# First four chunks of the hidden layer plain instead of two, and other places for the sums of squares

## Chip, cores and metric

The kernel runs on one core of one Trainium2 chip. The metric is the device time of one execution in microseconds (us), lower is better. Engines: TensorE (PE, its weight loads PEld), VectorE (DVE), ScalarE (ACT), GpSimd (POOL), SyncE (SP, which issues all DMAs here).

## What is computed

A decoder trunk on 512 tokens with model width 1024, in float32. Two layers; each has a SwiGLU feed-forward network (FFN) before and one after its mixer. The first mixer is a multi-scale causal pooling, the second a multi-head latent attention that reads one shared latent K/V. All reads of the residual h go through an RMSNorm.

```
def swiglu(u, wg, wu, wd):
    return (jax.nn.silu(u @ wg) * (u @ wu)) @ wd
...
    for l in range(DEPTH):
        h = h + 0.5 * swiglu(rmsnorm(h, ffn_pre_norm[l]), ...)
        u = rmsnorm(h, mix_norm[l])
        h = h + (pool_mixer(u, ...) if l < N_A_LAYERS else mla_attention(u, ...))
        h = h + 0.5 * swiglu(rmsnorm(h, ffn_post_norm[l]), ...)
        if l == N_A_LAYERS - 1:
            k_nope, k_rope, v = mla_shared_kv(h, ...)
    return rmsnorm(h, final_norm)
```

## The kernel before

Everything is kept transposed: h is eight tiles of 128 channels x 512 tokens. Each float32 product is made of three fp32r matmuls (`mm3`, lines 115 to 119): high by high, high by low, low by high part. So each weight is cast to its high part on ACT (L144, L178) and subtracted to its low part on DVE (L145, L179), and each input is split in the same way: high on ACT (L303), low on DVE (L308).

**RMSNorm.** The gain goes into the split of h; the root of the mean square is applied afterwards, to the products. `Norm.square` makes squares on ACT (the last one on DVE, L318), `Norm.accumulate` adds them on POOL into `sq_acc` (L325). `token_sums` (L239) sums over the partitions on TensorE: sixteen matmuls of one column, first operand `sq_acc`, then `sq`. `rsqrt` (L250 to L257) is eleven tiny instructions on DVE. `on_all` makes a diagonal on DVE (L280), spreads it over all partitions by a matmul of 512 columns (L287), and ACT copies it to `rb` (L289). `norm.r()` is sums and root, `norm.spread(r)` is `on_all`.

**FFN.** The hidden width 2816 is 22 chunks of 128. The first N_FIRST = 2 chunks are "plain": eight channels of input times gate and up weights (four products of 512 columns and 128 channels per channel, weights in four units of 512 KB, `wfirst`), accumulated in four PSUM tiles. From chunk 2 on, a chunk's gate and up product is made Strassen-like, with seven products of half size (p1 to p7: 84 matmuls of 256 columns). `group_weights` loads two tiles (`wgu`) and forms the sums of weight blocks with four additions on POOL (L191), splitting four tiles on the way; the split tiles come from `wsplit` (four buffers, shared with `load_w`), `wb` (two) and `wf` (two). The input side needs the operands `t1`, `t2`, `t4` (`Quarters.prepare`, L382 to L407) and `t3` (`prepare_t3`, L400 to L407), which overwrites the right half of the first four channels' split inputs; so it must come after the last plain product that reads these. p4 and p3 of a chunk run in the next chunk's loop.

`gated` (plain) or `p3` (Strassen) gives the hidden activation, which is split and kept (`mids`, eight chunks). The down product takes four chunks at a time: `down_steps(g)` says which columns d of the output are made in the loop of chunk g, `early` (between p2 and p4) or `late` (behind p7). `down_tail` is the rest. `DOWN_ORDER` fixes the order of the weights in memory. `on_h` is called when an output column is final; it starts the next norm's splits and squares.

TensorE's order is that of the program inside `manual_schedule`; the order of all other engines, and of TensorE outside, comes from a planner that simulates the program.

**Where the sums stand before.** In an FFN, behind the first of the four units (two channels): sums and root; behind the second: the spread and t3. In the pool stage (line 635): behind all four products of the first pair. Shared K/V (line 692): sums, root and spread by the planner's order, in front of `shared_kv`. At the end: the last two output columns are made in two token halves; behind the first half come its sums, root, spread, eight products on POOL (L942) and four DMAs, behind the second half sums, transposes and output.

Of the kernel before, what the change touches and what calls it, by code (L numbers as in the profile page):

```python
# [16 lines left out]
P = 128  # L17
T = 512
D = 1024
# [3 lines left out]
HT = T // 2  # L23
N_FIRST = 2
PART = 4
# [17 lines left out]
def down_steps(g):  # L43


    i, base = g % PART, g - g % PART - PART
    if base < 0:
        return [], []
    most, end, whole = range(base, base + PART - 1), [base + PART - 1], range(base, base + PART)
    if i == 0:  # L50
        return [], [(d, most, True, False) for d in range(2)]
    early = [(d, end, False, True) for d in range(2)] if i == 1 else []
    return early, [(d, whole, True, True) for d in (2 * i, 2 * i + 1)]
# [15 lines left out]
def trunk_kernel(  # L69
# [36 lines left out]
    def f(ap):  # L106
        return ap.bitcast(F32)
# [309 lines left out]

    def ffn(idx, norm, on_h, first=None, last=False):
        with tc.tile_pool(name="mid", bufs=1) as midp, tc.tile_pool(name="wb", bufs=2) as wb, \
# [108 lines left out]
            for u in range(ND // 2):  # L528
# [4 lines left out]
                if u == 0:  # L533
                    r = norm.r()
                    quarters = norm.quarters
                    quarters.prepare(ND // 2 - 1)
                elif u == 1:
                    rb = norm.spread(r)
                    for k in range(ND // 2):
                        quarters.prepare_t3(k)  # L540
            for j in range(2):
                gated(j, ps[2 * j], ps[2 * j + 1])

# [32 lines left out]
            for th in range(2 if last else 0):  # L576
                for step in down_tail()[-2:]:
                    down(*step, ts=slice(th * HT, (th + 1) * HT))


# [11 lines left out]
    with tc.tile_pool(name="pool", bufs=1) as pp:  # L592
# [41 lines left out]
        with tc.manual_schedule(engines={mybir.EngineType.PE}):  # L634
            os = {(0, tb): product(0, tb) for tb in range(NQB)}
            r = rms(norm.squares, D)
            for tb in range(2):
# [20 lines left out]

    def shared_kv(mean, rb):
        w = [part(load_w(wdkv[u]), 4, 256) for u in range(2)]  # L660
        o, orope = mm_tile(), mm_tile()
        with tc.tile_pool(name="kvw", bufs=2) as kw:
            for c in range(ND):
                x = split_gain(h[c], G_KV, c, kw, "kvh")
                mm3(o, [a[:, c % 4, :P] for a in w[c // 4]], x, c == 0, c == ND - 1)
                mm3(orope, [a[:, c % 4, P:] for a in w[c // 4]], x, c == 0, c == ND - 1)
            kr = kw.tile([P, T], F32, tag="kvr", name="kvr", bufs=1)
# [18 lines left out]
            nc.vector.tensor_tensor(out=krl[:64], in0=kr[:64], in1=f(krh[:64]), op=ALU.subtract)  # L686
            nc.sync.dma_start(f(krh[64:]), f(krh[:64]))

    class Shared:


        def __init__(self, norm):
            mean = mean_of(token_sums(norm.squares), D)
            self.base, self.gh, self.quarters = norm.base, norm.gh, norm.quarters
            self.rb = on_all(rsqrt(mean, "rms_r"))
            shared_kv(mean, self.rb)

# [236 lines left out]
    hg = [None] * ND  # L934

    def first_half():

        rb = final.rb(slice(0, half))
        for c in range(0, ND, 2):
# [22 lines left out]
    def on_h(c, ts):  # L962
        final.add(c, ts)
        if ts.start == 0:
            hg[c] = resid.tile([P, T], F32, tag=f"gh{c}_hi", name=f"hg{c}")
        nc.scalar.mul(hg[c][:, ts], h[c][:, ts], gain(G_FIN, c))
        if c == ND - 1:
            (second_half if ts.start else first_half)()

    ffn(3, norm, on_h, last=True)  # L970
    room.close()

# [92 lines left out]
```

## Time and profile before

| | |
|---|---|
| median of 2 runs | 1816.7 us (1815.43 to 1817.96) |
| profiled execution | 1818.21 us, its span 1816.4 us |
| mean granted TensorE clock | 0.974 of 2.4 GHz |
| TensorE busy, its weight loads | 95%, 86% |
| DVE, ACT, POOL busy | 73%, 48%, 34% |
| mean DMA rate | 92 GB/s |

In a row, the first figures are start and duration in us (timeline) or busy time and mean ns of one (groups); in brackets stands the idle time of the engine before the instruction and what ended it. A matmul's listed duration overlaps the next one's; the distance between starts is the pace.

### The profile page before, as it was taken

What the parts mean: (1) busy time and instruction counts of PE and PEld (TensorE: products, weight loads), DVE (VectorE), ACT (ScalarE), POOL (GpSimd) and SP (SyncE); (2) the same over time, 40 slices, a digit from 0 to 9 for tenths busy, and PEclk for the clock granted to TensorE, in tenths of its full rate; (3) what the DMA queues carried; (4) which work ended last, traced back from release to release, by engine and by line L of the source; (5) the groups of instructions that cost most, each with busy time, mean ns of one, the idle gap of its engine ahead of it and who ended that gap; (6) DMA issues with size and microseconds to landing.
All of it is one profiled execution on the core that took longest, in us unless ns stands there. A gap on an engine that the chain in (4) does not pass through costs nothing.

```text
span 1816.4 us, 28079 instructions
## 1 busy us (share of the span) xinstructions
PE 1725.0 (95%) x11088; PEld 1570.9 (86%) x11088; DVE 1329.3 (73%) x2121; ACT 869.1 (48%) x1428; POOL 610.0 (34%) x424
## 2 busy tenths in 40 slices
PE   4999999996999999989999999999999889999997
PEld 3899999985999999978999999878887679999996
DVE  8677777678777777789777777787665867777774
ACT  5444444454444444454444444576664534444443
POOL 4333333224333333233333332412121323333322
PEclk7999999998999999999999999999999889999998
DMA  4233333321233333222333333321221123333321
GB/s 151 86 101 105 105 105 105 105 84 34 94 105 105 105 101 99 93 70 87 105 105 105 105 105 99 94 69 52 83 82 47 58 82 105 104 100 99 97 90 48
DMA packets 49590, 166.83 MB, mean 92 GB/s; under 512 B 6320, under 2 KB 6320, under 8 KB 49456
## 3 DMA queue, kind: packets, MB, share of 16 engines
q1 hardware_dynamic: 49456, 165.02, 28.6%
q8 instruction: 87, 1.43, 0.3%
q14 instruction: 47, 0.39, 0.1%
HBM read 158.44 MB, written 2.10 MB: 88 GB/s over the span
## 4 chain that ended last, share of the span: by engine, by line
PE 86%; DVE 9%; ACT 2%; issue 2%; POOL 1%; DMA 1%; SPq 0%; DVEq 0%; POOLq 0%; ACTq 0%
PE mm L117 20%; PE mm L119 20%; PE mm L118 20%; PE aux L117 7%; PE aux L118 7%; PE aux L119 7%; DVE wlo L179 1%; DVE gh_lo L308 1%; DVE t_lo L407 1%; DVE wlo L145 1%; PE mm L831 1%; DVE b L401 1%; PE mm L830 1%; PE aux L867 1%; PE mm L832 0%
## 5 line engine op out<-in xcount | busy, mean ns | idle before, releaser
L191 POOL TENSOR_TENSOR wraw<-wraw 128x512 f32<-128x512 f32 x320 | 482.3, 1508 | 803.9 <-DVE flo L179 689.7
L117 PE MATMUL mm<-gh_hi,whi 128*128 128x256 f32 (+1 forms) x1424 | 425.9, 299 | 7.6 <-ACT whi L144 7.5
L118 PE MATMUL mm<-gh_lo,whi 128*128 128x256 f32 (+1 forms) x1424 | 423.5, 297 | 0.0
L119 PE MATMUL mm<-gh_hi,wlo 128*128 128x256 f32 (+1 forms) x1424 | 422.6, 297 | 0.0
L178 ACT CAST whi<-wraw 128x1024 fp32r<-128x1024 f32 x240 | 252.0, 1051 | 251.1 <-POOL wraw L191 205.4
L179 DVE TENSOR_TENSOR wlo<-wraw,whi 128x1024 fp32r<-128x1024 f32 x240 | 297.7, 1242 | 32.0 <-ACT whi L178 31.8
L117 PEld LDWEIGHTS mm<-gh_hi,whi 128*128 128x128 f32 x1424 | 276.2, 194 | 18.3 <-ACT whi L144 7.5
L118 PEld LDWEIGHTS mm<-gh_lo,whi 128*128 128x128 f32 x1424 | 275.8, 194 | 10.6 <-issue 1.5
L119 PEld LDWEIGHTS mm<-gh_hi,wlo 128*128 128x128 f32 x1424 | 275.4, 193 | 7.2 <-issue 0.2
L117 PE MATMUL aux<-mh,whi 128*128 128x512 f32 x576 | 225.3, 391 | 0.0
L118 PE MATMUL aux<-ml,whi 128*128 128x512 f32 x576 | 225.2, 391 | 0.0
L119 PE MATMUL aux<-mh,wlo 128*128 128x512 f32 x576 | 224.1, 389 | 0.0
L119 PE MATMUL mm<-t_hi,wlo 128*128 128x256 f32 x640 | 184.1, 288 | 10.1 <-DVE wlo L179 10.1
L474 DVE TENSOR_TENSOR mm<-c,mm 128x256 f32<-128x256 f32 x80 | 34.2, 428 | 207.4 <-PE mm L119 207.4
L117 PE MATMUL mm<-t_hi,whi 128*128 128x256 f32 x640 | 183.6, 287 | 0.0
L118 PE MATMUL mm<-t_lo,whi 128*128 128x256 f32 x640 | 183.5, 287 | 0.0
L145 DVE TENSOR_TENSOR wlo<-wraw,whi 128x1024 fp32r<-128x1024 f32 (+2 forms) x142 | 164.3, 1157 | 22.8 <-ACT whi L144 22.4
L144 ACT CAST whi<-wraw 128x1024 fp32r<-128x1024 f32 (+2 forms) x172 | 145.5, 863 | 55.9 <-PE mm L118 31.4
L432 ACT COPY c<-mm 128x256 f32<-128x256 f32 x240 | 88.6, 370 | 130.1 <-PE mm L119 130.1
L119 PEld LDWEIGHTS mm<-t_hi,wlo 128*128 128x128 f32 x640 | 125.4, 196 | 10.9 <-DVE wlo L179 10.9
L487 DVE TENSOR_TENSOR gate<-gate,rb 128x512 f32<-128x512 f32 x88 | 130.4, 1482 | 3.5 <-ACT gate L486 3.5
L119 PEld LDWEIGHTS aux<-mh,wlo 128*128 128x128 f32 x576 | 108.2, 188 | 23.2
(209 smaller groups left out, 3428.8 us busy)
## 6 DMA issues: line engine op xcount, KB each, us to landing
wraw<-in_wgu SPq DMA_DIRECT2D x160, 512.0 KB, 3.6
wraw<-in_wd SPq DMA_DIRECT2D x88, 512.0 KB, 3.6
wraw<-in_wo SPq DMA_DIRECT2D x16, 512.0 KB, 3.7
wraw<-in_wfirst SPq DMA_DIRECT2D x12, 512.0 KB, 3.6
wraw<-in_wheads SPq DMA_DIRECT2D x8, 512.0 KB, 3.5
h<-in_xT SPq DMA_DIRECT2D x8, 256.0 KB, 5.4
wraw<-in_wfirst SPq DMA_DIRECT2D x8, 256.0 KB, 5.4
qr<-yh SPq DMA_DIRECT2D x32, 64.0 KB, 2.0
```

The lines of the kernel that those rows point to most:

```text
L117: nc.tensor.matmul(out, w[0], x[0], start=start, stop=False, **kw)
L118: nc.tensor.matmul(out, w[0], x[1], start=False, stop=False, **kw)
L119: nc.tensor.matmul(out, w[1], x[0], start=False, stop=stop, **kw)
L144: nc.scalar.copy(hi[:, s], raw[:, s])
L145: lo_engines[i % len(lo_engines)].tensor_tensor(out=lo[:, s], in0=raw[:, s], in1=f(hi[:, s]), op=ALU.subtract)
L178: nc.scalar.copy(hi[:, s], raw[:, s])
L179: nc.vector.tensor_tensor(out=lo[:, s], in0=raw[:, s], in1=f(hi[:, s]), op=ALU.subtract)
L191: nc.gpsimd.tensor_tensor(out=out, in0=x, in1=y, op=ALU.add)
L308: nc.vector.scalar_tensor_tensor(out=lo, in0=h[c], scalar=gain(self.base, c), in1=f(hi), op0=ALU.mult, op1=ALU.subtract)
L432: nc.scalar.copy(t, acc[g]["x"])
L474: nc.vector.tensor_tensor(out=y, in0=act[g]["c16"], in1=y, op=ALU.add)
L487: nc.vector.tensor_tensor(out=gate, in0=gate, in1=rb, op=ALU.mult)
```

## The change

N_FIRST becomes 4: chunks 2 and 3 are plain too, with weights from the `wgu` units of these chunks (the up weights' two halves of channels lie in swapped order there). Chunk 2 is done gate first, then up; chunk 3 "by channel", gate and up alternating. Sums and root stand behind all eight channels of chunks 0 and 1, the spread behind chunk 2's gate, `gated` of chunks 0 and 1 with it; t3 is prepared when chunk 3 is through channel 3. The first down columns' first three chunks, `late` in chunk 4 before, become `early` there. In the pool stage the sums stand behind two of four products. `shared_kv` gets its own manual order with the sums behind channel 4. At the end, the first half's sums stand behind column 6 of the second half (`last`), its spread and output behind the last column.

```diff
-N_FIRST = 2
+N_FIRST = 4
...
-    if base < 0:
-        return [], []
     most, end, whole = range(base, base + PART - 1), [base + PART - 1], range(base, base + PART)
     if i == 0:
-        return [], [(d, most, True, False) for d in range(2)]
+        steps = [(d, most, True, False) for d in range(2)]
+        return (steps, []) if base == 0 else ([], steps)
...
                 if u == 0:
-                    r = norm.r()
                     quarters = norm.quarters
                     quarters.prepare(ND // 2 - 1)
-                elif u == 1:
+            r = norm.r()
+            ws = [part(load_w(wgu[idx, 0, m]), ND, P) for m in range(2)]
+            for m in range(2):
+                o = mm_tile()
+                for c in range(ND):
+                    mm3(o, [x[:, (c + 4 * m) % ND] for x in ws[m]], norm.gh[c], c == 0, c == ND - 1)
+                ps.append(o)
+                if m == 0:
                     rb = norm.spread(r)
+                    for j in range(2):
+                        gated(j, ps[2 * j], ps[2 * j + 1])
+            gated(2, ps[4], ps[5])
+
+            ws = [part(load_w(wgu[idx, 1, m]), ND, P) for m in range(2)]
+            ps = [mm_tile() for _ in range(2)]
+            for c in range(ND):
+                for m in range(2):
+                    mm3(ps[m], [x[:, (c + 4 * m) % ND] for x in ws[m]], norm.gh[c], c == 0, c == ND - 1)
+                if c == ND // 2 - 1:
                     for k in range(ND // 2):
                         quarters.prepare_t3(k)
-            for j in range(2):
-                gated(j, ps[2 * j], ps[2 * j + 1])
+            gated(3, *ps)
...
                     down(*step, ts=slice(th * HT, (th + 1) * HT))
+                    if th == 1 and step[0] == ND - 2:
+                        last()
...
-            os = {(0, tb): product(0, tb) for tb in range(NQB)}
-            r = rms(norm.squares, D)
+            os = {(0, tb): product(0, tb) for tb in range(2)}
+            ss = token_sums(norm.squares)
+            os.update({(0, tb): product(0, tb) for tb in range(2, NQB)})
+            r = rsqrt(mean_of(ss, D), "rms_r")
...
-            for c in range(ND):
-                x = split_gain(h[c], G_KV, c, kw, "kvh")
-                mm3(o, [a[:, c % 4, :P] for a in w[c // 4]], x, c == 0, c == ND - 1)
-                mm3(orope, [a[:, c % 4, P:] for a in w[c // 4]], x, c == 0, c == ND - 1)
+            with tc.manual_schedule(engines={mybir.EngineType.PE}):
+                for c in range(ND):
+                    x = split_gain(h[c], G_KV, c, kw, "kvh")
+                    mm3(o, [a[:, c % 4, :P] for a in w[c // 4]], x, c == 0, c == ND - 1)
+                    mm3(orope, [a[:, c % 4, P:] for a in w[c // 4]], x, c == 0, c == ND - 1)
+                    if c == 4:
+                        mean = mean_of(token_sums(norm.squares), D)
+            rb = on_all(rsqrt(mean, "rms_r"))
...
+    def first_sums():
+        firsts.append(final.r(slice(0, half)))
     def first_half():
-        rb = final.rb(slice(0, half))
+        rb = on_all(firsts.pop())
...
-        if c == ND - 1:
-            (second_half if ts.start else first_half)()
+        if c == ND - 1 and ts.start:
+            first_half()
+            second_half()
```

## Rows read from the trace of the kernel before

**Rows 1.** The page, busy us, share of the span and instructions of each engine.
```profile
PE 1725.0 (95%) x11088; PEld 1570.9 (86%) x11088; DVE 1329.3 (73%) x2121; ACT 869.1 (48%) x1428; POOL 610.0 (34%) x424
```

**Rows 2.** Waits of TensorE: us in total, times, longest us.
```profile
PE aux L239 <- POOL sq_acc L325: 28.7, 5, 12.3
...
PE aux L239 <- DVE sq L318: 17.8, 4, 6.2
...
PE aux L287 <- DVE diag L280: 10.9, 5, 4.3
...
PE mm L119 <- DVE wlo L179: 10.1, 4, 2.6
...
PE mm L117 <- DVE pvl L359: 4.4, 1, 4.4
```

**Rows 3.** Timeline of TensorE, head of FFN 0.
```profile
7.51 0.79 PE L117 MATMUL mm<-gh_hi,whi 128*128 128x512 f32 x1 [7.51 <-ACT whi L144]
...
27.32 0.59 PE L239 MATMUL aux<-ones,sq_acc 128*128 128x1 f32 x2 [12.30 <-POOL sq_acc L325]
...
36.54 0.77 PE L117 MATMUL mm<-gh_hi,whi 128*128 128x512 f32 x1
...
46.34 1.12 PE L287 MATMUL aux<-diag,ones 128*128 128x512 f32 x2 [1.51 <-DVE diag L280]
...
58.23 0.28 PE L117 MATMUL mm<-gh_hi,whi 128*128 128x256 f32 x1
...
68.30 0.28 PE L117 MATMUL mm<-t_hi,fhi 128*128 128x256 f32 x1
```

**Rows 4.** Timeline of TensorE, FFN 3: first and 24th plain, first Strassen matmul.
```profile
1427.67 0.39 PE L117 MATMUL mm<-gh_hi,whi 128*128 128x512 f32 x1
...
1432.88 0.39 PE L119 MATMUL mm<-gh_hi,wlo 128*128 128x512 f32 x1
...
1470.89 0.28 PE L117 MATMUL mm<-gh_hi,whi 128*128 128x256 f32 x1
```

**Rows 5.** Timeline of TensorE, FFN 1: first plain and first Strassen matmul.
```profile
412.11 0.45 PE L117 MATMUL mm<-gh_hi,whi 128*128 128x512 f32 x1
...
454.87 0.28 PE L117 MATMUL mm<-gh_hi,whi 128*128 128x256 f32 x1
```

**Rows 6.** Costliest groups by form: busy us, mean ns, idle before.
```profile
L191 POOL TENSOR_TENSOR wraw<-wraw 128x512 f32<-128x512 f32 x320 | 482.3, 1508 | 803.9 <-DVE flo L179 689.7 <-DVE wlo L179 45.0 <-issue 34.2
...
L179 DVE TENSOR_TENSOR wlo<-wraw,whi 128x1024 fp32r<-128x1024 f32 x240 | 297.7, 1242 | 32.0 <-ACT whi L178 31.8
```

**Rows 7.** Timeline of DVE, heads of FFN 0, 1 and 3.
```profile
30.39 0.68 DVE L145 TENSOR_TENSOR wlo<-wraw,whi 128x512 fp32r<-128x512 f32 x1
...
42.71 1.21 DVE L255 TENSOR_TENSOR rms_t<-rms_r,mean 128x4 f32<-128x4 f32 x1
...
44.34 0.16 DVE L255 TENSOR_TENSOR rms_t<-rms_r,mean 128x4 f32<-128x4 f32 x1
...
428.44 0.74 DVE L308 SCALAR_TENSOR_TENSOR gh_lo<-h,g_sb,gh_hi 128x512 fp32r<-128x512 f32 x1
...
1442.19 0.74 DVE L308 SCALAR_TENSOR_TENSOR gh_lo<-h,g_sb,gh_hi 128x512 fp32r<-128x512 f32 x1
```

**Rows 8.** Timeline of TensorE, FFN 2: shared K/V sums, first Strassen matmul.
```profile
786.72 0.59 PE L239 MATMUL aux<-ones,sq_acc 128*128 128x1 f32 x2 [5.43 <-POOL sq_acc L325]
...
825.17 0.28 PE L117 MATMUL mm<-gh_hi,whi 128*128 128x256 f32 x1
```

**Rows 9.** Stretches: busy us of each engine, granted clock, DMA share, GB/s.
```profile
58.20:90.00 31.80, 29.16 (x230) 28.93 (x229) 23.18 (x33) 14.29 (x23) 12.31 (x8) 0.95 0.26 84
...
384.00:412.00 28.00, 23.59 (x187) 23.27 (x186) 21.73 (x37) 17.00 (x27) 5.15 (x4) 0.94 0.31 97
```

**Rows 10.** Timeline of TensorE and POOL, tail of the kernel.
```profile
1798.51 1.22 PE L287 MATMUL aux<-diag,ones 128*128 128x256 f32 x2 [2.95 <-DVE diag L280]
...
1800.22 5.57 POOL L942 TENSOR_TENSOR y<-hg,rb 128x256 f32<-128x256 f32 x8 [6.84 <-ACT rb L289]
```

More of the change, by code (lines that the diff above doesn't have):

```diff
@@ L416, in operand, with ffn @@
             return [x[:, half * HT:(half + 1) * HT] for x in tiles]
-    def ffn(idx, norm, on_h, first=None, last=False):
+    def ffn(idx, norm, on_h, first=None, last=None):
         with tc.tile_pool(name="mid", bufs=1) as midp, tc.tile_pool(name="wb", bufs=2) as wb, \
@@ L657, in trunk_kernel, with shared_kv @@
     nc.gpsimd.memset(f(krl[64:]), 0.0)
-    def shared_kv(mean, rb):
+    def shared_kv(norm):
         w = [part(load_w(wdkv[u]), 4, 256) for u in range(2)]
@@ L687, in shared_kv @@
             nc.sync.dma_start(f(krh[64:]), f(krh[:64]))
+        return rb
     class Shared:
         def __init__(self, norm):
-            mean = mean_of(token_sums(norm.squares), D)
             self.base, self.gh, self.quarters = norm.base, norm.gh, norm.quarters
-            self.rb = on_all(rsqrt(mean, "rms_r"))
-            shared_kv(mean, self.rb)
+            self.rb = shared_kv(norm)
         def r(self):
@@ L934, in trunk_kernel @@
     hg = [None] * ND
+    firsts = []
+    def first_sums():
+        firsts.append(final.r(slice(0, half)))
     def first_half():
-        rb = final.rb(slice(0, half))
+        rb = on_all(firsts.pop())
         for c in range(0, ND, 2):
@@ L966, in on_h @@
         nc.scalar.mul(hg[c][:, ts], h[c][:, ts], gain(G_FIN, c))
-        if c == ND - 1:
-            (second_half if ts.start else first_half)()
-    ffn(3, norm, on_h, last=True)
+        if c == ND - 1 and ts.start:
+            first_half()
+            second_half()
+    ffn(3, norm, on_h, last=first_sums)
     room.close()
```

## Prediction

> **What bounds the kernel now.** I read the page's busy shares first: TensorE is busy for 95% of the span [rows 1], so only its idle time and its extra columns can move the end. Next the waits of TensorE: almost all of its waiting is with a few causes, each hit once per stage [rows 2]. The token sums wait for the accumulated squares on POOL (28.7 us) and for the last square on DVE (17.8), the spreading product waits for its diagonal (10.9), weights for the channel products arrive late (10.1), and the pool stage waits once (4.4). Together 71.9 us. Then TensorE's timeline at the head of each FFN shows what such a wait costs in full. In FFN 0 the sums begin at 27.32 after 12.30 us idle, the next products start at 36.54, the spreading product at 46.34, and the 96 products of the first two chunks, begun at 7.51, are through at 58.23 [rows 3].
>
> Two spacings are needed. From 1427.67 to 1432.88 lie 23 steps between 512-column matmuls [rows 4]: 0.2265 us each. From 58.23 to 68.30 lie the 84 matmuls of one Strassen chunk, 256 columns each [rows 3]: 0.120 us each. So 96 products of 512 columns need 21.7 us. Measured were 50.7 in FFN 0 (58.23 - 7.51), 42.8 in FFN 1 (454.87 - 412.11) [rows 5] and 43.2 in FFN 3 (1470.89 - 1427.67) [rows 4]. The excess is 29.0, 21.1 and 21.5 us. Of it some 2.3 is work that stays in any order: sixteen small matmuls of the sums and the two of the spread. 26.7, 18.8 and 19.2 us, together 64.7, are waits and the half-speed clock after them.
>
> **The change part by part.**
>
> *Chunks 2 and 3 plain.* A plain chunk is 48 matmuls by 0.2265 = 10.87 us, a Strassen chunk 84 by 0.120 = 10.08. Two chunks in four FFNs: 8 x 0.79 = **+6.3 us**, all on TensorE's path. The Trainium skill, "TensorE: Matmul & The Clock Gate", section "Back-to-back issue gap", gives an isolated gap of N/2.4 + 2.5 ns, 215.8 and 109.2 ns here; by that the term would be 8 x 1.19 = 9.5. The rows show about 11 ns more for each matmul of either width, and the rows decide.
>
> What these chunks no longer need is off the path: per chunk two splits fewer on DVE (1.24 us each for 1024 columns) and four additions fewer on POOL (1.51 each) [rows 6]. As many weight bytes are loaded as before, four 512 KB units per FFN by SP, only without the additions. I cost this at nothing; it is the margin that lets the rest work.
>
> *The sums behind the eight channels of chunks 0 and 1, the spread behind chunk 2's gate.* This attacks the 64.7. TensorE now goes on with channels 2 to 7 as soon as their low parts are written, and reaches the sums 72 matmuls (16.3 us) later. What is late next is DVE, which makes those low parts:
> - FFN 0: the last weight split runs 30.39 to 31.07, the twelve matmuls of its channel follow, so the products end at 33.8 at best [rows 7], against 7.51 + 21.7 = 29.2. That is 4.6 us that stay; with the half-speed start and a few short gaps I leave 7.5.
> - FFN 1: the last low part is done at 429.18 [rows 7], when TensorE, from 412.11 without a stop, is at channel 6; its end at 433.8 is hardly touched. I leave 0.5.
> - FFN 3: the last low part is done at 1442.93 [rows 7]; channel 7 would be reached at 1427.67 + 84 x 0.2265 = 1446.7. Nothing stays.
> - The spread: between the end of the sums (36.54) and the spread (46.34) lay 9.8 us [rows 3], as the root's small instructions stand behind DVE's backlog. Chunk 2's gate covers 24 x 0.2265 = 5.4. Bounds per FFN: 0 (the backlog has drained, since DVE gets 16 us longer) to 4.4. I take 1.5, nearer to the lower end because three of DVE's heaviest jobs, the t3 operands, now come later still. Three FFNs: 4.5 stay.
>
> So 64.7 - 7.5 - 0.5 - 4.5 = **-52.2 us**.
>
> *FFN 2* has its sums inside the shared K/V. They wait 5.43 us there, and from 786.72 to 825.17 lie 144 products of 512 columns [rows 8]: 32.6 us plus 2.3 for sums and spread, so 3.5 is lost to the slow clock. Sums after channel 4 of K/V can save up to 8.9; but the K/V inputs need eight low parts more from the same loaded DVE before anything else can start. Bounds 0 to 8.9, I take the middle, **-4.5**.
>
> *The late weights of the channel products.* In each FFN the third Strassen group waits once on a split, 10.1 us in four [rows 2]. The stretch around it ran at 0.95 of the clock for 31.8 us [rows 9], thus 3.2 us at half speed, which costs 1.6. Four times 2.5 + 1.6 plus 0.2 each of pipeline drain: 17.3. The reason is that the third group's small block takes a buffer that the first group frees only in the second one's loop, and POOL's four additions (6.0 us) with the splits follow. Now the 24 matmuls of group 5's `late` columns stand between, 24 x 0.2265 = 5.4 us of cover for a wait of 2.6: it goes. In its place comes a new one. The early `down` of group 4 needs a unit of wd, whose split buffer only chunk 3 frees; it must be cast and split (1.24 on DVE [rows 6]; for the cast on ACT I take the same) while p1 and p2 run, 24 x 0.120 = 2.9 us, and DVE has chunk 3's gating and the t3 operands at the same time. Bounds 0 to 6 per FFN; I take 2, including the clock. Sum: 17.3 - 8.0 = **-9.3**.
>
> *Pool stage.* The sums go in front of two of the four products, so the root starts 24 x 0.120 = 2.9 us earlier and 2.9 us more of products lie behind it. The wait of 4.4 [rows 2] and the clock of 0.94 over 28 us [rows 9], worth 1.7, make 6.1 at most. DVE then leads through the eight h updates; I take **-4**.
>
> *Tail.* The spread of the first half waited 2.95 us at 1798.51; now the last column's second half runs in that time. POOL's eight products for the first half took 5.57 us from 1800.22 [rows 10] and stood before the second half's sums; afterwards they run beside the second half's root chain, which is what is late next. Bounds 0 to 5 us, I take **-3**. On that chain: with POOL busy a tiny DVE instruction took 1.21 us, after it 0.16 [rows 7]. The Trainium skill, "SBUF — State Buffer", section "Who interferes with whom", says that a DVE instruction with two SBUF inputs and a GpSimd one that reads SBUF exclude each other for a whole instruction. By that the chain would take up to 5 us more here and the tail gains nothing; the rows agree with the rule, and it is the lower bound that I use.
>
> Sum: +6.3 - 52.2 - 4.5 - 9.3 - 4 - 3 = -66.7. The profiled execution took 1818.21 us (span 1816.4 and 1.8 around it; the median of the two timed runs, 1816.7, lies 1.5 below): 1818.2 - 66.7 = 1751.5, **1752 us**.
>
> **Rivals.**
> 1. *The wait moves to the spread and to group 4.* If DVE's backlog isn't drained, the spread waits 4.4 and the clock falls again (some 2 us) in three FFNs, 19.2 instead of 4.5, and the early unit costs 5 instead of 2 in four: 14.7 + 12 = 26.7 us less gain, 1778. For it: 9.8 us from sums to spread. Against it: two plain chunks take work off DVE and POOL.
> 2. *Every wait goes.* DVE is ahead everywhere: the 4.5 and the 8.0 vanish and FFN 2 gives its 8.9: 17 us more, 1735. For it: the late rows of low parts lie ahead of TensorE's need in FFN 1 and 3. Against it: FFN 0's DVE row.
> 3. *Group 4 starves (the other side).* Before, the waiting at the head let ACT, DVE and POOL split two groups ahead. If that lead was bought by the wait, TensorE reaches groups 4 to 6 with no weights ready: each then runs at the pace of buffer release, two splits, two additions, a split, two additions, a split, about 14 us of chain (four casts and splits near 1.2 each, four additions at 1.5) for 10 us of products, beside t3 and four gatings on the same DVE. The gain is used up when this costs 66.7 / 4 = 16.7 us more per FFN than I allow; at 20 it gives 1831. For it: the two demands do meet in one stretch. Against it: the chain starts when buffers fall free in chunk 2, 11 to 16 us before group 4.
> 4. *DVE's order decides.* Only TensorE's order is written by hand. If the planner puts chunk 2's and 3's splits and the t3 work ahead of the low parts, half of the 52.2 stays: 1778.
>
> **How the numbers follow.** The forecast has 0.60 (its own range 1738 to 1770), rival 1 0.15, rival 2 0.10, rival 4 0.10, rival 3 0.05. The range 1734 to 1788 holds the forecast, rivals 1, 2 and 4 about their centres, and leaves out rival 3 and the outer tails. A change of 2% (36 us, below 1780.4 of the median) is about what a measurement of this kernel tells from no change: faster 0.83 (forecast, rival 2, most of 1 and 4), same 0.12, slower 0.05.
>
> **What would show it.** Right: no L239 row on TensorE waits over 2 us in FFN 0, 1 and 3; first channel product of FFN 1 some 47 us behind its first plain product (192 products, sums, spread), where four chunks are done; the granted clock near full in these stretches; no wait of 2.6 us on wlo in the third group. Wrong: waits of 4 us or more under L287, new waits of L117 to L119 on the wd unit or t3 in group 4, or low parts (L308) ending the waits of the plain products.

## The result, and the profile after the change

The changed kernel takes 1753.5 us (median of two runs, 1752.56 to 1754.46), 0.9652 of the kernel before, with a 95% interval of 0.9611 to 0.9694: faster, and 1.5 us from the forecast. The profiled execution took 1754.46 us with a span of 1752.7; that is 3.0 us above the 1751.5 that the prediction's sum gave for it. As will be seen, the sum came out better than its terms: some of them were off by more than 10 us, and that they cancelled was luck.

In the changed file the lines up to L521 carry a number one lower (L239 is L238, L287 is L286, L308 is L307), the last ones a number 26 higher (L942 is L968).

The page's busy times, and the row of the granted clock over 40 slices, answering to [rows 1]:

```profile
PE 1709.3 (98%) x10800; PEld 1542.9 (88%) x10800; DVE 1298.3 (74%) x2065; ACT 849.9 (48%) x1388; POOL 565.6 (32%) x392
...
PEclk9999999999999999989999999999999999999998
```

TensorE is at 98% where it was at 95. It has 288 matmuls fewer (8 chunks, 84 - 48 each), POOL 32 additions and DVE 56 instructions fewer.

The waits of TensorE (us in total, times, longest), answering to [rows 2]:

```profile
PE aux L286 <- DVE diag L279: 8.7, 3, 5.2
...
PE mm L116 <- ACT kvh_hi L347: 4.8, 1, 4.8
PE mm L117 <- DVE kvh_lo L348: 3.7, 1, 3.7
...
PE mm L118 <- DVE wlo L144: 1.6, 2, 1.2
```

Three of the four largest rows of before, the sums behind POOL, the sums behind DVE and the late weights (L179), are gone. The spread's row is smaller, but one of its waits is longer than any of before. And there is a new pair, the operands of the shared K/V (kvh).

TensorE's timeline at the sums and the spread, in FFN 0 and in FFN 3:

```profile
7.92 0.79 PE L116 MATMUL mm<-gh_hi,whi 128*128 128x512 f32 x1 [7.92 <-ACT whi L143]
...
33.57 0.28 PE L238 MATMUL aux<-ones,sq_acc 128*128 128x1 f32 x2
...
46.21 2.07 PE L286 MATMUL aux<-diag,ones 128*128 128x512 f32 x2 [5.20 <-DVE diag L279]
...
1385.51 0.39 PE L116 MATMUL mm<-gh_hi,whi 128*128 128x512 f32 x1
...
1407.27 0.28 PE L238 MATMUL aux<-ones,sq_acc 128*128 128x1 f32 x2
...
1414.63 1.12 PE L286 MATMUL aux<-diag,ones 128*128 128x512 f32 x2
```

In FFN 3 the 96 products take 21.8 us (1407.27 - 1385.51), the spacing's own 21.7, and the spread comes without a wait. In FFN 0 they take 25.7 (33.57 - 7.92), and the spread waits 5.2.

**The time by stage.** Milestones of TensorE's timeline cut both spans. A head of an FFN goes from its first plain product to the first of the 24 `late` down matmuls of group 5; the K/V and FFN 2 go from FFN 1's last tail product to the same point; the pool stage from FFN 0's last tail product to FFN 1's first; the tail begins behind the last tail product of 512 columns. The forecast column puts the prediction's steps on these stages (an FFN's share of the plain chunks is +1.58, of the late weights -2.33).

```
stage              before    after   change   forecast
start to FFN 0       7.51     7.92    +0.41      0
head of FFN 0       98.01    81.16   -16.85    -18.45
pool stage          27.61    21.95    -5.66     -4
head of FFN 1       89.83    72.28   -17.55    -17.55
K/V and FFN 2       94.75    93.86    -0.89     -5.25
attention          273.02   271.38    -1.64      0
head of FFN 3       90.50    69.18   -21.32    -18.45
tail                27.19    27.00    -0.19     -3
rest              1107.98  1107.97    -0.01      0
span              1816.40  1752.70   -63.70    -66.7
```

Nearly all of the gain, 61.4 of 63.7 us, lies where the prediction put most of it: in the heads of three FFNs and in the pool stage. FFN 2 and the tail, which were to give some 8, give nearly nothing. What attention shows is no work of the change; the last section comes to it.

### The profile page after: what moved, and what is told of

The parts are those of the page before. It is cut to its first block, busy times and chain, and to the rows that moved or that the text cites. A ratio compares the mean times of both kernels' runs of the same rounds, so it can differ in the third digit from the quotient of the medians.

```text
span 1752.7 us, 27363 instructions
## 1 busy us (share of the span) xinstructions
PE 1709.3 (98%) x10800; PEld 1542.9 (88%) x10800; DVE 1298.3 (74%) x2065; ACT 849.9 (48%) x1388; POOL 565.6 (32%) x392
## 5 line engine op out<-in xcount | busy, mean ns | idle before, releaser
L190 POOL TENSOR_TENSOR wraw<-wraw 128x512 f32<-128x512 f32 x288 | 438.4, 1522 | 776.4 <-DVE flo L178 682.3
L118 PE MATMUL mm<-gh_hi,wlo 128*128 128x256 f32 (+1 forms) x1424 | 433.7, 305 | 1.6 <-DVE wlo L144 1.6
L177 ACT CAST whi<-wraw 128x1024 fp32r<-128x1024 f32 x216 | 227.0, 1051 | 226.1 <-POOL wraw L190 184.2
L178 DVE TENSOR_TENSOR wlo<-wraw,whi 128x1024 fp32r<-128x1024 f32 x216 | 267.5, 1239 | 3.3 <-ACT whi L177 3.3
L144 DVE TENSOR_TENSOR wlo<-wraw,whi 128x1024 fp32r<-128x1024 f32 (+2 forms) x158 | 183.3, 1161 | 36.6 <-ACT whi L143 35.3
L143 ACT CAST whi<-wraw 128x1024 fp32r<-128x1024 f32 (+2 forms) x188 | 162.2, 879 | 82.5 <-PE mm L117 56.8
L118 PE MATMUL mm<-t_hi,wlo 128*128 128x256 f32 x576 | 163.0, 283 | 0.0
L117 PE MATMUL mm<-t_lo,whi 128*128 128x256 f32 x576 | 163.0, 283 | 0.0
L116 PE MATMUL mm<-t_hi,whi 128*128 128x256 f32 x576 | 163.0, 283 | 0.0
L324 POOL TENSOR_TENSOR sq_acc<-sq_acc,sq 128x512 f32<-128x512 f32 (+1 forms) x43 | 63.6, 1479 | 197.3 <-ACT sq L320 196.9
```

Source lines behind the costliest of these rows:

```text
L116: nc.tensor.matmul(out, w[0], x[0], start=start, stop=False, **kw)
L117: nc.tensor.matmul(out, w[0], x[1], start=False, stop=False, **kw)
L118: nc.tensor.matmul(out, w[1], x[0], start=False, stop=stop, **kw)
L143: nc.scalar.copy(hi[:, s], raw[:, s])
L144: lo_engines[i % len(lo_engines)].tensor_tensor(out=lo[:, s], in0=raw[:, s], in1=f(hi[:, s]), op=ALU.subtract)
L177: nc.scalar.copy(hi[:, s], raw[:, s])
```

## The experiments

Each ran on one chip together with the kernel before, which took 1818.4 to 1819.7 us there. The first run to read is the changed kernel itself.

**The changed kernel again** (no edit).

> The changed kernel again, unedited, beside the others on the same chip: ratio 0.965 to the kernel before, and the same stretches within 1 us but for the first transfers at the start (7 to 8.4 us in the other runs).

Measured: 1755.1 us, ratio 0.9646 (0.9633 to 0.9659). Every stage from FFN 0's head on lies within 0.2 us of the table; the start took 7.12. In the kernels that follow, stages that an edit does not touch differ somewhat more: by up to 0.9 us in FFN 2's, by up to 0.4 in the tail, and FFN 0's head, which begins with the first transfers, once by 1.5. So smaller differences of one stage are not read as an edit's. 0.9646 is the ratio that the others are held against.

**The sums back at their old place**, the chunks plain:

```diff
                 if u == 0:
+                    r = norm.r()
                     quarters = norm.quarters
                     quarters.prepare(ND // 2 - 1)
-            r = norm.r()
+                elif u == 1:
+                    rb = norm.spread(r)
...
                 if m == 0:
-                    rb = norm.spread(r)
                     for j in range(2):
```

> The changed kernel (four plain chunks) with the sums of FFN 0, 1 and 3 back behind channels 0 and 1 and the spread back behind channels 2 and 3. Theory: the place of the sums makes the gain: the waits under the sums' line come back and with them some 52 to 65 us: 1807 to 1819. Rival: the two plain chunks, which take splits from DVE and additions from POOL, made most of it: below 1780, with waits under the sums' line of less than half of before (46.5 us).

Measured: 1788.0 us, ratio 0.9833 (0.9817 to 0.9849), so 34 us above the changed kernel. Neither 52 us nor "most of it by the plain chunks": it fell between the two theories. The waits of TensorE in this kernel:

```profile
PE aux L238 <- POOL sq_acc L324: 17.7, 2, 11.5
PE aux L238 <- DVE sq L317: 16.9, 3, 7.2
...
PE aux L286 <- DVE diag L279: 1.8, 1, 1.8
```

The sums' waits are back, all in the three heads, with 34.6 us; before had 39.3 there (46.5 by [rows 2], less 5.4 in FFN 2 and 1.8 in the tail). The spread's are not: of 10.9 only the tail's 1.8 is left. So the plain chunks alone remove the spread's waits in the FFNs, the late weights, and a small part of the sums' waits, 4.7 us. What they remove of the spread's in the three heads is 6.7 us: the 1.5 of [rows 3] in FFN 0 and, in the kernel before, these two in FFN 1 and FFN 3:

```profile
442.98 1.12 PE L287 MATMUL aux<-diag,ones 128*128 128x512 f32 x2 [0.88 <-DVE diag L280]
...
1456.29 2.08 PE L287 MATMUL aux<-diag,ones 128*128 128x512 f32 x2 [4.26 <-DVE diag L280]
```

**The other half alone**: two plain chunks as before, the sums behind all eight channels, the spread behind the first two Strassen products.

```diff
-                    r = norm.r()
                     quarters = norm.quarters
...
-                elif u == 1:
-                    rb = norm.spread(r)
-                    for k in range(ND // 2):
-                        quarters.prepare_t3(k)
-            for j in range(2):
-                gated(j, ps[2 * j], ps[2 * j + 1])
+            r = norm.r()
...
                 p2(g)
+                if g == N_FIRST:
+                    rb = norm.spread(r)
...
```

(The last part also holds the gating of chunks 0 and 1 and the t3 operands.)

> The kernel before (two plain chunks) with one edit: sums of FFN 0, 1 and 3 behind all eight channels, spread, gating and the t3 operands behind the first two products of the first Strassen group. Theory: the sums' waits go, but only 2.9 us of products lie between sums and spread, where 9.8 are needed in FFN 0: spread waits of 5 to 8 us and the clock's fall after them, some 10 us in each of three FFNs, so half of the 52 to 57 us is kept: 1785 to 1795. Rival: no cover is needed and the plain chunks only cost their 6.3 us: 1760 to 1768. Other rival: DVE, with the operands of the Strassen products ahead of it, is late for the first group in any order, and nothing is won: 1810 or more.

Measured: 1810.3 us, ratio 0.9955 (0.994 to 0.997): 8 us won. That is the number of the "other rival", and its reason, DVE with other work ahead, is close too. The waits, and DVE's timeline in FFN 3, where the sums are through at 1445.04:

```profile
PE aux L287 <- DVE diag L280: 45.9, 5, 16.6
PE mm L119 <- DVE wlo L179: 10.1, 4, 2.6
```

```profile
1451.04 2.28 DVE L179 TENSOR_TENSOR wlo<-wraw,whi 128x1024 fp32r<-128x1024 f32 x1
1453.24 0.15 DVE L265 TENSOR_SCALAR mean<-aux 128x4 f32<-128x4 f32 x1
1455.55 1.23 DVE L179 TENSOR_TENSOR wlo<-wraw,whi 128x1024 fp32r<-128x1024 f32 x1 [2.16 <-ACT whi L178]
1456.69 0.16 DVE L250 TENSOR_SCALAR rms_t<-mean 128x4 int32<-128x4 int32 x1
```

The sums' waits are gone in the three heads, and nearly their whole price is paid one step later, at the spread. DVE keeps the order it was given: the mean stands behind t3 operands and weight splits for 8.2 us (1453.24 - 1445.04), and then a split, itself waiting 2.16 us for ACT, stands between the mean and the root's first instruction. The third group's late weights stay, with 10.1.

The three heads in the four kernels, from the same milestones:

```
                                FFN 0    FFN 1    FFN 3    sum against before
before                          98.01    89.83    90.50
plain chunks, sums early        92.86    84.51    80.34    -20.6
two plain, sums late            96.10    87.88    87.32     -7.0
changed kernel (both)           81.16    72.28    69.18    -55.7
```

The two parts alone make 27.7 us, together 55.7. The half that is missing belongs to neither. DVE's timeline above shows why: the late sums need the shorter queues that the plain chunks make. One thing more differs: between sums and spread lie 24 products of 256 columns here (2.9 us) and 24 of 512 in the changed kernel (5.4). That accounts for at most 7.7 us in the three heads, where the spread waits 41.7.

**Which queue?** The prediction costed what the plain chunks take off POOL and DVE at nothing. In FFN 3's head of before, DVE's groups by shape (busy us, mean ns) hold this row:

```profile
L308 DVE SCALAR_TENSOR_TENSOR gh_lo<-h,g_sb,gh_hi 128x512 fp32r<-128x512 f32 x4 | 5.0, 1254 | 0.0
```

With four plain chunks and early sums the same four instructions read:

```profile
L307 DVE SCALAR_TENSOR_TENSOR gh_lo<-h,g_sb,gh_hi 128x512 fp32r<-128x512 f32 x4 | 2.9, 739 | 0.0
```

The mean of the same work is 0.5 us shorter; in before two of the four take 0.74 us as here, and two take 1.75 and 1.79. What is missing beside it is POOL's additions for the Strassen groups: in before, six of them lie between 1431.77 and 1451.96, 8.5 us in all. So the next kernel puts POOL work back into the kernel of the sums' old place, 12 additions in each of three FFNs whose result goes nowhere:

```diff
...
+                    for _ in range(3 if c >= ND // 2 and idx != 2 else 0):
+                        nc.gpsimd.tensor_tensor(out=scrap, in0=scrap, in1=f(norm.gh[c][0])[:, :256], op=ALU.add)
...
```

> The kernel with four plain chunks and the sums at their old place (1788.0 us in the earlier run, ratio 0.983), with 12 additions of 128x256 on POOL that nobody needs at the head of FFN 0, 1 and 3, some 0.7 us each, so about 8.6 us of POOL in each, about as much as the two Strassen groups' additions put there before. Theory: a good part of what the plain chunks win beside their own price is that these additions are gone, which stand ahead of the squares on POOL and beside which DVE's small blocks take up to twice as long: the heads of the three FFNs (92.9, 84.5 and 80.3 us) grow by 3 to 8 us each, and the time is 1797 to 1810. Rival: what counts is DVE's own shorter list (fewer splits, t3 later), and POOL has room: each head within 1.5 us of these values, 1788 to 1792.

Measured: 1805.6 us, ratio 0.9925 (0.9908 to 0.9941), 17 us more. POOL's and DVE's groups, the first over the whole run, the second from 1421.3 to 1442.0 in FFN 3:

```profile
L535 POOL TENSOR_TENSOR scrap<-scrap,gh_hi 128x256 f32<-128x256 f32 x36 | 36.4, 1011 | 2.0
```

```profile
L309 DVE SCALAR_TENSOR_TENSOR gh_lo<-h,g_sb,gh_hi 128x512 fp32r<-128x512 f32 x4 | 3.8, 975 | 0.0
```

12.1 us of POOL work in each head made the heads 5.5, 6.6 and 3.8 us longer (98.32, 91.11 and 84.16), 15.9 together, and DVE's blocks grew from 0.739 to 0.975 us in the mean. The sums' waits rose from 34.6 to 51.8 us:

```profile
PE aux L240 <- DVE sq L319: 29.1, 3, 11.4
PE aux L240 <- POOL sq_acc L326: 22.7, 3, 14.2
```

So additions on POOL do lengthen these waits, and most of the 17.2 us more, 12.2, is waiting for the last square, which DVE makes. But the 15.9 us are not a share of the 20.6 that the plain chunks had won by themselves: this load is larger than before's and lies at other moments, and the sums' waits now exceed before's 39.3, of which the plain chunks had taken only 4.7. The spread did not start to wait, so POOL does not make that part. What is left as its cause is DVE's own list, which the plain chunks shorten; no run takes that alone.

**The place of the early down steps.**

```diff
-        return (steps, []) if base == 0 else ([], steps)
+        return [], steps
```

> The changed kernel with one word of the order taken back: the first down steps of the fifth group stand behind its seven products, not between its second and third. Theory: the third group's wait went because the late columns stand ahead of it, and the early place costs and brings nothing: 1754.5 within 1.5. By the step of the prediction the early unit costs 2 us in each FFN, which goes: 1747. Rival: the early place is what covers the weights of the first Strassen group, and its wait of 2.6 us with the slow clock (some 4 us each) comes back in every FFN: 1770.

Measured: 1753.9 us, ratio 0.9646 (0.9631 to 0.966): no difference. Neither the 2 us per FFN of the prediction nor the rival's cover exists; the third group's wait stays away without the early place.

**The shared K/V.**

```diff
-    def shared_kv(norm):
+    def shared_kv(mean, rb):
...
-                    if c == 4:
-                        mean = mean_of(token_sums(norm.squares), D)
-            rb = on_all(rsqrt(mean, "rms_r"))
...
```

(The sums and the spread stand ahead of the products again, and TensorE's order there is the planner's.)

> The changed kernel with the shared K/V alone taken back (sums ahead of the K/V products, spread left to the planner). By the step of the prediction the move was worth 4.5 us: 1759. By the reading of the trace the wait only changed its cause (5.43 us for the accumulated squares before, 4.78 for the first K/V operand and 3.65 for its low part after, on the same rows of ACT and DVE): 1754.5 within 1.5 either way, with a wait of some 5 us for the squares at the head of FFN 2 again.

Measured: 1753.6 us, ratio 0.9644 (0.9628 to 0.966): no difference in the time (the stage takes 92.5 us against 93.9, and attention the 1.6 more that the last section tells of). TensorE's first wait there is the old one again:

```profile
746.50 0.58 PE L238 MATMUL aux<-ones,sq_acc 128*128 128x1 f32 x2 [5.47 <-POOL sq_acc L324]
```

So the change took away a wait that hid another, of 4.8 us. ACT makes the first kvh behind the end of FFN 1's products although it needs only h. Its pool is opened where FFN 1's middle operands lay. The next kernel puts these operands into buffers that stand free:

```diff
-                    x = split_gain(h[c], G_KV, c, kw, "kvh")
+                    x = [room.act.tile([P, T], F32R, tag=tag, name=f"kvh_{s}", bufs=3) for s, tag in (("hi", "g"), ("lo", "m"))]
+                    nc.scalar.mul(x[0], h[c], gain(G_KV, c))
...
```

> The changed kernel with one edit: the two operands of each K/V product (kvh) lie in buffers that stand free (those of g and m), not in a pool opened where FFN 1's middle operands lay. Theory: in FFN 2 the waits of 4.8 and 3.6 us under the K/V products are waits for that memory, since its last readers are the last products of FFN 1; with it the operands are made beside these products and both waits go, with the slow clock behind them: the stretch from FFN 1's last tail product to FFN 2's late columns, 88.8 us, loses 6 to 10, and the time is 1745 to 1749. Rival: ACT and DVE are simply busy with FFN 2's own operands in that order, and the wait stays or moves to the sums, which wait for the last square: 1753 or more.

Measured: 1748.3 us, ratio 0.961 (0.9597 to 0.9623); the stage takes 87.5 us, 6.4 less. TensorE's timeline there, and ACT's row of the first two operands, at 745.62 in the changed kernel:

```profile
740.77 0.39 PE L116 MATMUL mm<-kvh_hi,whi 128*128 128x512 f32 x1
743.64 0.70 PE L117 MATMUL mm<-kvh_lo,whi 128*128 128x512 f32 x1 [2.48 <-DVE kvh_lo L685]
```

```profile
730.92 1.32 ACT L684 ACTIVATE kvh_hi<-h,g_sb 128x512 fp32r<-128x512 f32 x2
```

The memory was the cause: with nothing but the buffers changed, the operands are made 15 us earlier. (There are three buffers now and not two; for the first two operands that can't matter.) By which way it works is not shown: in the changed kernel FFN 1's last product ends at 741.61, and ACT, before it makes kvh at 745.62, still does a split, a square and a cast from 743.53 on, in the planner's order. What is late next is their low part, behind DVE's other work, with 2.48.

**The pool stage.**

```diff
-            os = {(0, tb): product(0, tb) for tb in range(2)}
-            ss = token_sums(norm.squares)
-            os.update({(0, tb): product(0, tb) for tb in range(2, NQB)})
-            r = rsqrt(mean_of(ss, D), "rms_r")
+            os = {(0, tb): product(0, tb) for tb in range(NQB)}
+            r = rms(norm.squares, D)
```

> The changed kernel with the pool stage alone taken back: all four products of the first pair ahead of the sums. If the edit itself made the stage's 5.6 us (27.4 us before, 21.8 after, from the last tail product to FFN 1's first product), the stage takes 27.4 again and the time is 1760. If part of it came from the emptier queues that the new FFN 0 leaves behind, the loss is 2 us or less: 1756.

Measured: 1757.1 us, ratio 0.9661 (0.9646 to 0.9675). The profiled execution, with a span of 1753.1, is at the fast end of its runs; by the ratios the edit is worth 2.7 us (0.0015 of 1818). The stage takes 25.0 us: 3.0 of its 5.7 are this edit's, of which FFN 1's head gives 1.0 back (71.25). The other 2.6 came with the rest of the change. Two plain chunks with late sums leave the stage at 28.2, and four with early sums and the pool stage's edit have it at 22.1, close to the changed kernel's 21.9, so it is the plain chunks'. By which engine wasn't tried.

**The tail.**

```diff
...
-        if c == ND - 1 and ts.start:
-            first_half()
-            second_half()
+        if c == ND - 1:
+            (second_half if ts.start else first_half)()
```

(The first half's sums go back to their old place with it.)

> The changed kernel with the tail's edit alone taken back: spread and eight POOL products of the first half stand ahead of the second half's last column again. By the step of the prediction that tail was worth 3 us: 1754.5 + 3 = 1757.5 in the profiled execution. By the reading of the changed kernel's trace (the root chain of the second half takes 5.75 us beside POOL's products, where it took 2.33 before, and the first half's stores stand among the second half's in SP's queue) the edit gained nothing: 1754.5, within 1 either way, with TensorE idle for 2.9 us ahead of the first half's spread and the second chain back at 2.3 us.

Measured: 1754.7 us, ratio 0.9649 (0.9635 to 0.9664), tail 27.38 against 27.00. The kernel with the early K/V operands, whose tail is the changed kernel's, shows 27.4 too, so no gain of the edit can be told from none. In the changed kernel, POOL's eight products and the second half's root on DVE read:

```profile
1738.34 5.51 POOL L968 TENSOR_TENSOR y<-hg,rb 128x256 f32<-128x256 f32 x8 [4.21 <-ACT rb L288]
```

```profile
1738.89 0.16 DVE L264 TENSOR_SCALAR mean<-aux 128x2 f32<-128x2 f32 x1 [1.79 <-PE aux L238]
1739.08 0.70 DVE L249 TENSOR_SCALAR rms_t<-mean 128x2 int32<-128x2 int32 x1
...
1743.22 0.65 DVE L255 SCALAR_TENSOR_TENSOR rms_t<-rms_t,rms_r 128x2 f32<-128x2 f32 x1
1743.90 0.16 DVE L256 SCALAR_TENSOR_TENSOR rms_r<-rms_t,rms_r 128x2 f32<-128x2 f32 x1
```

From 1739.08 to 1743.87, as long as POOL works, seven instructions on two numbers per partition take 0.64 to 0.70 us each; then 0.16. The next kernel takes POOL out: the first half is transposed and scaled as the second is.

```diff
-        rb = on_all(firsts.pop())
...
-                nc.gpsimd.tensor_tensor(out=y[:, i], in0=hg[c + i][:, :half], in1=rb, op=ALU.mult)
+        r = firsts.pop()
...
+                    nc.tensor.transpose(
+                        out=o[:, i * P:(i + 1) * P], in_=hg[4 * quarter + i][:, tb * P:(tb + 1) * P],
+                        identity=ident)
...
+                nc.scalar.mul(y, o, r[:, tb:tb + 1])
...
```

> The changed kernel with the first half of the output made as the second is: transposed by TensorE, scaled by ACT, so no spread, no diagonal and no POOL product at the end. Theory (DVE's small instructions wait for POOL's): the second half's root chain takes 2.3 us instead of 5.75, the spread's 1.8 us of TensorE goes and the stores no longer mix: 5 to 7 us faster, 1748 to 1749.5. Rival (the chain is slow for another reason, such as the transposes beside it on TensorE): the small instructions still take 0.65 us each and the gain is at most 2 us: 1752.5 or more.

Measured: 1750.6 us, ratio 0.9629 (0.9614 to 0.9644); the tail takes 23.1 us, 3.9 less. The same chain of DVE:

```profile
1740.49 0.17 DVE L249 TENSOR_SCALAR rms_t<-mean 128x2 int32<-128x2 int32 x1
...
1742.46 0.16 DVE L256 SCALAR_TENSOR_TENSOR rms_r<-rms_t,rms_r 128x2 f32<-128x2 f32 x1
```

All 11 take 0.16 or 0.17: with the mean 2.3 us instead of 5.75. The transposes run beside it as they did before, so the rival is out. The gain is short of 5 to 7, since the second half's sums now wait for an accumulator of the first half: they begin 6.1 us behind the start of the first half's last sum, not 4.8.

**The spread later**, in the middle of chunk 2's up product:

```diff
+                    if m == 1 and c == ND // 2 - 1:
+                        rb = norm.spread(r)
+                        for j in range(2):
+                            gated(j, ps[2 * j], ps[2 * j + 1])
                 ps.append(o)
-                if m == 0:
-                    rb = norm.spread(r)
...
```

> The changed kernel with the spread and the gating of chunks 0 and 1 in the middle of chunk 2's up product, 12 products later. Theory: the diagonal is late against TensorE in FFN 0 by 5.2 us and in FFN 1 by 1.7, so 2.7 us more of cover takes 2.7 and 1.7 off these waits and some 2 us of slow clock with them, and costs FFN 3 nothing: 1748 to 1751. Rival: all six accumulators are then taken when chunk 3 begins, which waits for the first gating, 2 to 3 us in each of four FFNs: 1757 or more.

Measured: 1749.4 us, ratio 0.962 (0.9606 to 0.9635). FFN 0's head takes 77.96 (-3.2), FFN 1's 70.92 (-1.4), FFN 3's 69.71 (+0.5), FFN 2's stage 94.38 (+0.5). The wait in FFN 0:

```profile
46.15 1.12 PE L286 MATMUL aux<-diag,ones 128*128 128x512 f32 x2 [1.31 <-DVE diag L279]
```

The diagonal comes at the same time as before; 12 more products of cover take its wait from 5.20 to 1.31. Chunk 3 waits for no accumulator. What the later place costs is small and shows elsewhere: the early down steps now wait for their weights, 1.24 us in FFN 2 (0.30 in the changed kernel), 0.83 in FFN 0 and 0.40 in FFN 3.

```profile
PE aux L118 <- DVE wlo L144: 2.7, 4, 1.2
```

**Three of these together**: the later spread, the early K/V operands, and the transposed first half, with the second half's sums between its two quarters and all its accumulators among the six large ones.

> The changed kernel with the later spread, the transposed first half (its accumulators now among the six large ones, the second half's sums between the two quarters) and the early K/V operands together. The three lie in different stages, so they should add: 5 from the spread, 4 from the tail and 2 more from sums that no longer wait for a buffer, 6 to 10 from K/V: 1754 - 17 to 21 = 1733 to 1737. If the K/V edit wins nothing: 1743.

Measured: 1738.4 us, ratio 0.9553 (0.9539 to 0.9566): 17 us faster than the changed kernel, at the lower end of 17 to 21; the time itself lies 1.4 us above the 1733 to 1737 expected. The stages add as they should (77.6, 70.9, 87.5 and 69.7 us, tail 20.3); attention took 273.0, the 1.6 more that is told of below. The span is 1736.8; behind the first transfer of weights, the largest waits left in the heads and in the shared K/V are these:

```profile
PE aux L286 <- DVE diag L279: 2.5, 1, 2.5
PE mm L117 <- DVE kvh_lo L685: 2.5, 1, 2.5
```

## Why the prediction came out right, and which steps did not

**The bound and the target: right.** TensorE's waits at the heads were what could be won, and 55.7 of the 63.7 us came from three heads, where the steps had 54.5. No sums' wait is left in FFN 0, 1 and 3, the third group's 2.6 us are gone, FFN 1's first channel product comes 49.5 us behind its first plain one (439.55 - 390.02, forecast 47), and the granted clock is 1.00 in the heads of FFN 1 and 3.

**Two terms of the wrong size that cancelled.** "Sums and spread" was put at -52.2, and what the plain chunks take off DVE and POOL "at nothing; it is the margin that lets the rest work". With the plain chunks in place, the place of the sums is worth 35.1 us in three heads (heads of 92.86, 84.51 and 80.34 against the changed kernel's); with two plain chunks it is worth 7.0. The plain chunks alone are worth 20.6, where their steps gave 2.3 (3 x (1.58 - 2.33)). The step that failed is the reading of the 64.7 us as one cause, the place of the sums: 11.4 us of these waits (4.7 of the sums', 6.7 of the spread's), and the slow clock behind them, go with the plain chunks alone. That additions on POOL can lengthen the sums' waits is shown by the run with the load; how much of before's they made is not.

That the sum held was luck. The plain chunks gave 18.3 us more than their steps: 6.0 of it is the early unit's allowance in three FFNs, which was not needed; the other 12.3, those 11.4 us of waits and some slow clock, was booked under the sums. The sums' place gave 17.1 less than its step: these 12.3 and 4.8 more, the larger part of them waits and slow clock in FFN 0 (below). The 6.0 that were not needed paid for the 4.8. The clause on the margin was right but not priced; the run with two plain chunks prices it: the spread then waits 16.6, 12.3 and 12.7 us. (What a plain chunk spares DVE was read a little too high: of its two splits one has 1024 columns and one 512, as L179's 240 and 80 of before become 216 and 72 while L145's 104 become 120; that is 1.9 us and not 2.5.)

**FFN 0: right in sum, not in its parts.** The products left 3.9 us behind (25.65 - 21.7), not 7.5 and even less than the 4.6 that the prediction held to be the least. The spread was to leave 1.5 and at most 4.4; it waited 5.2. From 47.30 to 52.09 the granted clock was 0.50, the lower level, and the 72 products behind the spread took 19.0 us instead of 16.3. The bounds came from how fast the backlog drains; what counted was the order within it. DVE in the changed kernel:

```profile
39.10 0.69 DVE L178 TENSOR_TENSOR flo<-wraw,fhi 128x512 fp32r<-128x512 f32 x1 [2.43 <-ACT fhi L177]
40.05 2.19 DVE L144 TENSOR_TENSOR wlo<-wraw,whi 128x1024 fp32r<-128x1024 f32 x1 [0.26 <-ACT whi L143]
42.16 0.15 DVE L264 TENSOR_SCALAR mean<-aux 128x4 f32<-128x4 f32 x1
42.35 1.04 DVE L249 TENSOR_SCALAR rms_t<-mean 128x4 int32<-128x4 int32 x1
```

The sums were through at 35.27. The mean started 6.9 us later, behind weight splits; for 2.43 us of that time DVE stood idle at a split whose source ACT had not made. This is close to rival 4, DVE's order, in one FFN: the splits stood ahead of the mean and not, as the rival had it, ahead of the low parts. The wait and the slow clock cost some 8 us together (5.2 and 2.7). This is also the one sign of "wrong" that came true in size, a wait of 4 us or more at the spread; a low part and the early unit's weights ended one wait each, of 0.3 us.

**FFN 1: right in sum** (-17.55 forecast and measured), with some luck: the products left 1.3 us behind (0.5 forecast) and the spread 1.7 (1.5), and the early unit's 2 were not needed. **FFN 3: 2.9 us better**, since two allowances were not used: the spread's 1.5 and the early unit's 2. The **early unit** (8 us in four FFNs) costs nothing in any of them; taken back, it changes nothing.

**FFN 2: -0.9 instead of -5.3.** The step took the middle of 0 to 8.9 and called the K/V inputs a reason for the lower end, but not why they are late. They are late because of the memory that FFN 1 holds to its end. The trace of before shows their lateness beside [rows 8]: ACT made the first two kvh from 785.25 to 786.58, while TensorE waited for the squares until 786.72.

**Pool stage:** right at -5.7 against -4 (the ceiling was 6.1), but the edit's own part is 3.0.

**Tail: -0.2 instead of -3.** Here the prediction named the right price and then took a value above it: a root chain beside POOL's products. Its instructions take 0.64 to 0.70 us beside POOL's products of 0.69 (5.51 / 8) and 0.16 without. The Trainium skill, "SBUF — State Buffer", section "Who interferes with whom", says that a DVE instruction with two SBUF inputs and a GpSimd one that reads SBUF exclude each other for a whole instruction; by that the tail gains nothing, and the trace agrees. The lower bound was the answer, as it had a row of the same kind behind it and the middle had none.

**Rivals.** Rival 1 (the wait moves to the spread) holds in FFN 0 alone, and in all three FFNs in the kernel with two plain chunks. Rival 2 did not occur; its 1735 is what the three repairs reach (0.9553 x 1816.7 = 1735.5). Rival 3 did not occur: from group 5's late columns on, every FFN takes the same time as before.

## What to carry to other kernels

Before a wait is booked to the order of one engine, look at what the engines it waits for are doing then: half of this change's gain exists only because its two halves came together, and each alone gave 20.6 and 7.0 of 55.7 us. Ask of a wait that is to go what else becomes ready at the same moment; in FFN 2 it was nothing for a while, and 4.8 us of waiting stood right behind the 5.4 that went. A short chain of small instructions that sets the end should not run beside GpSimd.

## What was not expected of the hardware

Small DVE instructions lose as much time as larger ones: beside POOL's instructions of 128x256, two int32 numbers per partition took 0.70 us instead of 0.17 in the tail, and a block of 128x512 (gh_lo) 1.21 instead of 0.74 in the run with the load. This holds for one-input instructions too (the shift at 1739.08), but not for the mean just before it: that one reads TensorE's sums and took 0.16 beside the same POOL work.

The clock can differ behind the same wait. At the end of attention TensorE runs the same products behind the same wait of 1.84 us in every kernel here. In the kernel before, and then in the changed one:

```profile
1396.79 0.50 PE L117 MATMUL mm<-pth,vh 128*128 128x512 f32 x1 [1.84 <-ACT pth L355]
...
1397.94 0.63 PE L119 MATMUL mm<-ah,wlo 128*128 128x512 f32 x1
1398.36 0.63 PE L117 MATMUL mm<-ah,whi 128*128 128x512 f32 x1
```

```profile
1356.26 0.50 PE L116 MATMUL mm<-pth,vh 128*128 128x512 f32 x1 [1.84 <-ACT pth L354]
...
1357.06 0.40 PE L118 MATMUL mm<-ah,wlo 128*128 128x512 f32 x1
1357.29 0.39 PE L116 MATMUL mm<-ah,whi 128*128 128x512 f32 x1
```

The spacing is 0.43 us in the one (granted clock 0.51 over 3.4 us, the lower level) and 0.23 in the other (1.00, the higher). Of 14 profiled executions, four fell to the lower level here (before, the K/V taken back, the POOL load, the three together) and ten did not: 1.6 us that belong to no edit. What decides it stays open.
